# Scale rows by a store to DRAM and a repeating load instead of products with the identity, and one turn of the stabiliser instead of four, in a one-layer encoder kernel

## The chip, the cores and the metric

The kernel runs on one core of one Trainium2 chip. The metric is the device time of one execution in microseconds (us), and its median over several runs. The core has five engines that run their own instruction streams in a fixed order: TensorE (PE in the profile), VectorE (DVE), ScalarE (ACT), GpSimd (POOL) and SyncE (SP), which issues nearly all DMA transfers of this kernel. An engine waits at an instruction until the semaphores it names have been raised; nothing behind it on that engine overtakes it.

## The reference

One layer over 2048 tokens of width 1024, in float32:

```python
xn = rms_norm(x, mix_norm_g)
aq, ak, av, mq, mk, mv, mo, i, f, ga, gm = split(xn @ w_in)
att = chunk_band_attention(aq, ak, av, rel_bias)          # 8 heads of 64, own chunk of 64 and 8 before
hm  = mlstm_chunkwise(silu(conv(mq)), silu(conv(mk)), mv, i + b_i, f + b_f)   # 4 heads of 128, running-max stabiliser
m   = sigmoid(mo) * headwise_rms_norm(hm)
y   = sigmoid(ga) * (att @ w_att_proj) + sigmoid(gm) * (m @ w_mlstm_proj)
x   = x + y @ w_out
x   = x + relu(rms_norm(x, ffn_norm_g) @ w_up) ** 2 @ w_down
out = rms_norm(x, final_norm_g)
```

`rms_norm(x, g)` is `x * rsqrt(mean(x * x) + 1e-6) * g` over the 1024 features of a token.

## The kernel before, in words

**Layout.** The 2048 tokens are four blocks (b = 0 to 3) of T = 512; two blocks are a span (s = 0, 1). Activations lie feature by token: a tile holds 128 features (its partitions) by 512 tokens. A value that belongs to a token, such as the scale of a norm, is then needed as a *row*: the same 512 numbers in each of the 128 partitions. It comes out of a sum over features as a *column*: a tile of 128 x 4, where partition p and column t hold token 128 t + p.

**Products.** Each float32 matrix product is made of three products of rounded parts. ACT rounds a tile into the high part and DVE subtracts it for the low part (`split_now`, lines 585 and 587, for weights; lines 1393 and 1398 for activations). The big products are done by a scheme with seven products in place of eight, with sums of weights that are made on the way and parked in DRAM (`wsum`). Weights flow through four raw tiles (`wraw`) and three split tiles (`wsp`), which PE uses in turn.

**Stages, by time.** The two first blocks' norms and their value products; the input projections of span 0 (`quad`, line 715) up to about 450 us, while the operands of span 1 are prepared (`take_x1`, line 1993, needs the rows of span 1); from 450 us the input products of span 1 (`product`, lines 746 and 751) beside the mixers of blocks 0 and 1, that is attention (lines 1625, 1657, 1550) and recurrence (1874 to 1939); then output projection, up-projection and down-projection (lines 646 to 648) of span 0 with the mixers of blocks 2 and 3 beside it (1450 to 1900 us); then the same for span 1, whose last block is turned to token by feature for its final norm (`down_turned`, line 1017; `turned`, `turned_out`).

**The four places that the change touches.**
- `rows_far(s)`: for each of the span's two blocks, waits for the column of scales `r_in` (the power -0.5 is done by POOL, line 1317 for span 0, line 1339 for span 1), then makes the row by four products of the column, repeated over 128 columns, with the identity (line 1352). ACT copies the bank into a `bias` tile (line 1355).
- `final_scale(s, h)`: the same for the final norm of blocks 0, 1 and 2: sums over features by four products with ones (line 2672), a scale on DVE (2675), the power on POOL (2679), four products with the identity (2683), a copy by ACT (2686). `final_put` then multiplies eight tiles by the row on DVE (2658) and sends them out.
- `turned(s, mid)` for block 3: loads the row of mean squares of the middle norm, `midd` (line 2613, in `final_mid`), squares it on ACT (2615), and turns it to a column by four products with ones (2522) and a scale on DVE (2525).
- `gates_rest(b)`: the stabiliser `mt`, a tile of 128 tokens by 16 (four groups of tokens by four heads), is turned to rows by four turns of 4 columns each (line 1806), copied by ACT as 4 x 512 (1809) and stored to DRAM (`mrow`), from where the recurrence loads a head's row for all partitions (`load_rec`, line 1835).

**What sets the order.** Every piece of work is a generator that yields the engine it wants next with an estimated duration (`yield "pe", 1080`). A planner (`Flow`) runs all generators once against estimated clocks, takes due times from that run, and runs them again to emit the instructions in planned order. A store or load yields 800 ns of the SP queue and some time until it counts as landed. So other costs, or other pieces of work, change the order of everything planned later, on all engines; the hardware then keeps that order.

Of the kernel before, what the change touches and what calls it, by code (L numbers as in the profile page):

```python
# [38 lines left out]
EPS = 1e-6  # L39
# [93 lines left out]
class Flow:  # L133
# [162 lines left out]
def act_ns(n, ps=False, ap=0):  # L296
    return (51 if ps else 93) + 0.834 * n + 93 * ap
# [16 lines left out]
class Layer:  # L314
# [1027 lines left out]
    def rows_far(self, s, ready, read):  # L1342

        fl, nc = self.fl, self.nc
        got = yield "get", self.bias, 2
        yield "wait", [self.ev_const]
        for b in range(2):
            yield "wait", [self.ev_r[2 * s + b]]
            (bk,) = yield "get", self.banks, 1
            yield "pe", 1080  # L1350
            for t in range(NT):
                nc.tensor.matmul(bk[:, t * P:(t + 1) * P], self.rin[2 * s + b][:, t:t + 1].to_broadcast([P, P]),
                                 self.ident, start=True, stop=True)
            yield "act", act_ns(512, True)
            nc.scalar.copy(got[b][:, :T], bk)
            fl.put(self.banks, bk)
            self.rows[b] = got[b][:, :T]
        fl.set(ready)
        yield "wait", read
        fl.put(self.bias, *got)  # L1360

    def square_in(self, b, k, x, tot, ev):

# [356 lines left out]
    def gates_rest(self, b, bk):  # L1720
        fl, nc, B, sm = self.fl, self.nc, self.blk[b], self.sm
        V = nc.vector
# [7 lines left out]
        e, d, s, s2, p = (sm[n] for n in ("e", "d", "s", "s2", "p"))  # L1730
# [30 lines left out]
        a, z = self.cum  # L1761
# [3 lines left out]
        while sh < P:  # L1765
            yield "dve", 150
            V.tensor_tensor(z[:, 64:], a[:, 64:], a[:, 64 - sh:192 - sh], op=ALU.max)
            a, z = z, a
# [4 lines left out]
                         start=True, stop=True)  # L1773
# [27 lines left out]
        V.tensor_scalar(ex[:, 1], ex[:, 1], 0.5, None, op0=ALU.mult)  # L1801
        yield "dve", 85
        V.tensor_scalar(ex[:, 2], ex[:, 2], C1, None, op0=ALU.mult)
        yield "pe~", 428
        for c in range(NT):
            nc.tensor.transpose(bk[:MH, c * P:(c + 1) * P], sm["mt"][:, c * MH:(c + 1) * MH], self.ident)
        (tmp,) = yield "get", self.temp, 1
        yield "act", act_ns(512, True)
        nc.scalar.copy(tmp[:MH, :512], bk[:MH])
        fl.put(self.banks, bk)  # L1810
        fl.set(B["gates"])
        fl.spawn(self.store(self.mtd.ap()[b], tmp[:MH, :512], B["rows"], self.temp, tmp), 1)

    def recurrence(self, b):
        fl, B = self.fl, self.blk[b]
# [663 lines left out]

    def final(self, s):  # L2480
        fl = self.fl
        tot, mid = yield "get", self.bias, 2
        fl.spawn(self.turned(s, mid), 2)
# [21 lines left out]
        fl.put(self.temp, sq)  # L2505
        fl.set(summed[j])

    def turned(self, s, mid):

        fl, nc = self.fl, self.nc  # L2510
        V = nc.vector
        yield "wait", [self.acc_done[s][4, 1], self.kept_ev]
        self.tgain = [g[:, :512] for g in (yield "get", self.temp, 2)]
        yield "sp", 1570, 2000
        for o in range(2):
            nc.sync.dma_start(self.tgain[o], self.io["grow"][:, o * 512:o * 512 + 512].to_broadcast([P, 512]))
        ev = Event()
        yield from self.final_mid(2 * s + 1, mid[:, :512], ev)
        (bk,) = yield "get", self.banks, 1
        yield "pe~", 900  # L2520
        for t in range(NT):
            nc.tensor.matmul(bk[:, 2 * t:2 * t + 2], mid[:, t * P:(t + 1) * P], self.ones, start=True, stop=True)
        r, sums = self.rr["z3"], self.rq
        yield "dve", 150
        V.tensor_scalar(r, bk[:, :2 * NT].rearrange("p (t a) -> p t a", a=2)[:, :, 0], 1.0 / D, None, op0=ALU.mult)
        fl.put(self.banks, bk)
        fl.put(self.bias, mid)
        done = [Event() for _ in range(2 * NT)]
        for o in (4, 0):
            for t in range(NT):  # L2530
                fl.spawn(self.turn_part(s, o, t, done[t + (4 - o)]), 2)
        yield "wait", done
        yield "dve", 150
        V.scalar_tensor_tensor(r, sums[:, 0], 1.0 / D, r, op0=ALU.mult, op1=ALU.add)
        fl.set(self.turned_ev)
# [130 lines left out]
    def final_scale(self, s, h, slot, summed, ready):  # L2666
        fl, nc = self.fl, self.nc
        yield "wait", summed
        (bk,) = yield "get", self.banks, 1
        yield "pe~", 900  # L2670
        for t in range(NT):
            nc.tensor.matmul(bk[:, 2 * t:2 * t + 2], slot[:, t * P:(t + 1) * P], self.ones, start=True, stop=True)
        r = self.rr[f"z{2 * s + h}"]
        yield "dve", 75
        nc.vector.tensor_scalar(r, bk[:, :2 * NT].rearrange("p (t a) -> p t a", a=2)[:, :, 0], 1.0 / D, None,
                                op0=ALU.mult)
        fl.put(self.banks, bk)
        yield "pool", 1900
        nc.gpsimd.tensor_tensor(r, r, self.half, op=ALU.pow)
        (bk,) = yield "get", self.banks, 1  # L2680
        yield "pe~", 1080
        for t in range(NT):
            nc.tensor.matmul(bk[:, t * P:(t + 1) * P], r[:, t:t + 1].to_broadcast([P, P]), self.ident,
                             start=True, stop=True)
        yield "act", act_ns(512, True)
        nc.scalar.copy(slot[:, :512], bk)
        fl.put(self.banks, bk)
        fl.set(ready)

    def late(self):  # L2690
# [11 lines left out]
    def build(self):  # L2702
        fl, nc = self.fl, self.nc
        E = lambda n: [Event() for _ in range(n)]
        f32d = lambda name, *shape: nc.dram_tensor(name, shape, F32, kind="Internal")
# [11 lines left out]
        self.xud = f32d("xu", 7, 4, P, T)  # L2717
        self.gated, self.mtd = f32d("gatepart", 40, T), f32d("mrow", NB, MH, T)
        self.rbd = f32d("relrow", AH, 512)
        self.fin_ev = [E(KT) for _ in range(2)]  # L2720
        self.fin = [f32d(f"fin{h}", KT, P, T) for h in range(2)]
        self.ud = f32d("u", 4, 7, 4, P, T)
# [18 lines left out]
        for b in range(NB):  # L2741
# [3 lines left out]
                mid=Event(), vo={}, vn={}, vp_ev=E(4), mvh_ev=E(MH), row_ev=E(MH), rows=Event(), gf=Event(), heads_left=[2] * 4))  # L2745
# [115 lines left out]
```

## Time and profile before

| | |
|---|---|
| median of 3 runs | 2727.39 us (2727.08 to 2732.34) |
| profiled execution: its span | 2725.8 us, first to last instruction |
| around the span | 2727.4 - 2725.8 = 1.6 us to the median |
| DMA | 678 MB, 249 GB/s over the span |
| granted TensorE clock | 0.999 |

How to read the views. The profile is of one execution. "Busy" is the time in which an engine had an instruction under way; on PE, products overlap, so two starts are closer together than a product is long. A row of instruction groups names the line of the kernel, engine and operation, output <- inputs by the program's tile names, shapes, count, busy time, mean duration in ns of one, and the idle time ahead of them with what ended it. A float32 product that is not split in parts shows as two records, so four products with the identity are "x8", and four turns are "x4". A row of waits reads: who waited <- for what: total us, times, longest. "[1.11 <-DVE ctx L2086]" behind a row of the timeline is idle time ahead of it and its releaser. "Us to landing" of a DMA is counted from its issue.

### The profile page before, as it was taken

The page shows a single profiled execution, that of the slowest core. Times are in us where ns is not written, and L with a number is a line of the kernel's source. Part 1 is how long each engine was busy: PE and PEld are TensorE (multiplying, and loading weights), DVE is VectorE, ACT ScalarE, POOL GpSimd, SP SyncE. Part 2 cuts the span into 40 slices and gives each one's busy share as a digit, 9 for nine tenths or more (in the row PEclk, how much of TensorE's full clock was granted, in tenths as well). Part 3 has the DMA queues.
Part 4 walks back from the last instruction along what each step waited for, and adds up shares of the span by engine and source line. Part 5 has one row for each costly group of instructions (what it writes and reads, how often), then busy time and mean ns, then how long its engine had stood idle before and what let it go on. Part 6 is the DMA issues. An engine that isn't in the chain of part 4 may idle for free.

```text
span 2725.8 us, 38104 instructions
## 1 busy us (share of the span) xinstructions
PE 2708.3 (99%) x12784; PEld 2253.3 (83%) x12784; DVE 2108.8 (77%) x3750; ACT 1542.1 (57%) x2685; POOL 48.0 (2%) x79
## 2 busy tenths in 40 slices
PE   9999999999999999999999999999999999999998
PEld 8878888888888887888888888888888888888887
DVE  7878876888877879987768888889798665657675
ACT  6545456776753645566556766656345565554443
POOL 0000000000000000000000000000000000000000
PEclk9999999999999999999999999999999999999999
DMA  8777889888877889867779787776864454578773
GB/s 305 275 258 277 301 286 293 272 242 275 262 234 238 270 302 321 286 214 265 266 236 288 244 257 225 240 232 220 276 227 160 163 197 159 189 271 285 274 239 134
DMA packets 336712, 678.29 MB, mean 249 GB/s; under 512 B 37396, under 2 KB 66708, under 8 KB 336516
## 3 DMA queue, kind: packets, MB, share of 16 engines
q1 hardware_dynamic: 335796, 674.80, 74.1%
q8 instruction: 100, 1.64, 0.3%
q10 hardware_dynamic: 720, 1.06, 0.1%
q14 instruction: 96, 0.79, 0.1%
HBM read 458.27 MB, written 214.30 MB: 247 GB/s over the span
## 4 chain that ended last, share of the span: by engine, by line
PE 86%; DVE 7%; DMA 3%; issue 2%; ACT 2%; SPq 0%; POOL 0%; ACTq 0%; POOLq 0%; DVEq 0%
PE bank L715 34%; PE bank L746 11%; PE bank L647 8%; PE bank L648 8%; PE bank L646 8%; PE bank L1181 3%; PE bank L751 2%; PE bank L1550 2%; PE bank L1625 2%; PE bank L1657 2%; DVE wsp L587 1%; PE bank L1017 1%; DMA tmp<-in_x 1%; DMA x<-ctx 1%; PE bank L1885 0%
## 5 line engine op out<-in xcount | busy, mean ns | idle before, releaser
L715 PE MATMUL bank<-r,wsp 128*128 128x512 f32 x4872 | 1111.3, 390 | 2.2 <-DVE ctx L2086 1.1
L715 PEld LDWEIGHTS bank<-r,wsp 128*128 128x128 f32 x4872 | 913.0, 188 | 195.0 <-DVE ctx L2086 3.5
L585 ACT CAST wsp<-wraw 128x1024 fp32r<-128x1024 f32 x437 | 459.1, 1051 | 491.4 <-PE bank L715 167.8
L587 DVE TENSOR_TENSOR wsp<-wraw,wsp 128x1024 fp32r<-128x1024 f32 x437 | 534.0, 1222 | 239.0 <-ACT wsp L585 233.7
L646 PE MATMUL bank<-r,wsp 128*128 128x512 f32 x960 | 379.3, 395 | 0.0
L648 PE MATMUL bank<-r,wsp 128*128 128x512 f32 x960 | 375.3, 391 | 0.0
L647 PE MATMUL bank<-r,wsp 128*128 128x512 f32 x960 | 375.2, 391 | 0.0
L746 PE MATMUL bank<-r,wsp 128*128 128x512 f32 x1512 | 368.6, 394 | 0.9 <-DVE ctx L941 0.7
L746 PEld LDWEIGHTS bank<-r,wsp 128*128 128x128 f32 x1512 | 279.0, 188 | 56.9 <-DVE ctx L941 1.6
L648 PEld LDWEIGHTS bank<-r,wsp 128*128 128x128 f32 x960 | 180.2, 188 | 38.5
L647 PEld LDWEIGHTS bank<-r,wsp 128*128 128x128 f32 x960 | 180.5, 188 | 33.4
L646 PEld LDWEIGHTS bank<-r,wsp 128*128 128x128 f32 x960 | 180.4, 188 | 33.5
L1398 DVE TENSOR_TENSOR r<-r 128x512 fp32r<-128x512 f32 x255 | 167.9, 684 | 20.6 <-ACT r L1393 20.0
L2086 DVE TENSOR_TENSOR ctx<-bank,ctx 128x512 f32<-128x512 f32 x174 | 118.9, 686 | 70.3 <-PE bank L715 67.5
L1393 ACT CAST r<-r 128x512 fp32r<-128x512 f32 x255 | 148.8, 617 | 33.4 <-DMA r<-u 30.4
L604 DVE TENSOR_TENSOR wraw<-wraw,wraw 128x1024 f32<-128x1024 f32 x112 | 136.4, 1218 | 4.3 <-DMA wsum<-wraw 3.3
L1638 ACT ACTIVATE sc<-sc,scs 128x640 f32<-128x640 f32 (+4 forms) x128 | 97.6, 763 | 67.5 <-DVE scs L1631 66.5
L2078 ACT COPY ctx<-bank 128x512 f32<-128x512 f32 x174 | 100.9, 583 | 61.0 <-PE bank L715 43.4
L2407 ACT ACTIVATE ctx<-ctx 128x512 f32<-128x512 f32 x96 | 60.6, 631 | 103.2 <-DVE ctx L2086 103.1
L1662 DVE TENSOR_TENSOR r<-bank,r 128x512 fp32r<-128x512 f32 (+1 forms) x168 | 95.7, 593 | 15.0 <-ACT r L1660 14.4
L1550 PE MATMUL bank<-r,r 128*128 128x512 f32 x336 | 94.8, 364 | 0.0
L1660 ACT CAST r<-bank 128x512 fp32r<-128x512 f32 (+1 forms) x168 | 81.0, 516 | 17.2 <-PE bank L1657 16.0
(267 smaller groups left out, 3253.3 us busy)
## 6 DMA issues: line engine op xcount, KB each, us to landing
wraw<-in_wf SPq DMA_DIRECT2D x196, 512.0 KB, 4.9
r<-u SPq DMA_DIRECT2D x224, 256.0 KB, 4.3
wraw<-wsum SPq DMA_DIRECT2D x104, 512.0 KB, 4.6
u<-ctx SPq DMA_DIRECT2D x128, 256.0 KB, 2.4
ctx<-in_wf SPq DMA_DIRECT2D x104, 256.0 KB, 4.4
wsum<-ctx SPq DMA_DIRECT2D x104, 256.0 KB, 4.2
u<-tmp SPq DMA_DIRECT2D x96, 256.0 KB, 2.7
ctx<-in_xt SPq DMA_DIRECT2D x64, 256.0 KB, 4.8
```

The costliest lines, as they stand in the source:

```text
L585: nc.scalar.copy(w[:, 0], raw)
L587: nc.vector.tensor_sub(w[:, 1], raw, w[:, 0].bitcast(F32))
L604: V.tensor_sub(dst, x, y)
L646: mm(ps, lh, rh, start=first, stop=False)
L647: mm(ps, lh, rl, start=False, stop=False)
L648: mm(ps, ll, rh, start=False, stop=last)
L715: mm(ps, wv[:, x, k, n], a[:, y], start=new and k == 0 and x == y == 0, stop=k == 3 and x == 1, skip_group_check=True)
L746: mm(ps, wv[:, x, k, n], a[:, y], start=start and x == y == 0, stop=stop and x == 1, skip_group_check=True)
L1393: self.nc.scalar.copy(dst[:, 0], src)
L1398: self.nc.vector.tensor_sub(dst[:, 1], src, dst[:, 0].bitcast(F32))
L1550: nc.tensor.matmul(bkv[:, :, c0:c0 + w], st, sl[:, :, o:o + w], start=n == 0, stop=n == total - 1)
L2086: nc.vector.tensor_add(t[:, o:o + 512], ps, t[:, o:o + 512])
```

## The change

Four edits:
1. `row_of`, a new helper, stores a column (128 x 4) to a row of 512 numbers in DRAM, `tokrow`, waits for that store, and loads the row into all 128 partitions. `rows_far` uses it for span 1 in place of the products with the identity (span 0 keeps them).
2. `final_scale` uses it for its three rows.
3. `turned` loads the row of `midd` straight as a column, and squares it on DVE with the factor EPS; the row load, the square on ACT, the four products with ones and the scale on DVE go, and so does the use of a second `bias` tile.
4. `gates_rest` turns all 16 columns of `mt` at once; ACT copies 16 x 128, and the store puts the pieces in place.

```diff
@@ rows_far
             yield "wait", [self.ev_r[2 * s + b]]
+            if s == 1:
+                yield from self.row_of(self.rin[2 + b], self.rowd.ap()[b:b + 1], got[b][:, :T])
+                self.rows[b] = got[b][:, :T]
+                continue
             (bk,) = yield "get", self.banks, 1
...
+    def row_of(self, r, row, to):
+        kept = Event()
+        yield from self.store(row.rearrange("o (t p) -> p (o t)", p=P), r, kept)
+        yield "wait", [kept]
+        yield "sp", 800, 2500
+        self.nc.sync.dma_start(to, row.to_broadcast([P, T]))
@@ gates_rest
-        yield "pe~", 428
-        for c in range(NT):
-            nc.tensor.transpose(bk[:MH, c * P:(c + 1) * P], sm["mt"][:, c * MH:(c + 1) * MH], self.ident)
+        yield "pe~", 107
+        nc.tensor.transpose(bk[:16, 0:P], sm["mt"], self.ident)
         (tmp,) = yield "get", self.temp, 1
-        yield "act", act_ns(512, True)
-        nc.scalar.copy(tmp[:MH, :512], bk[:MH])
+        yield "act", act_ns(128, True)
+        nc.scalar.copy(tmp[:16, :P], bk[:16, 0:P])
...
-        fl.spawn(self.store(self.mtd.ap()[b], tmp[:MH, :512], B["rows"], self.temp, tmp), 1)
+        fl.spawn(self.store(self.mtd.ap()[b].rearrange("h (c p) -> c h p", p=P), tmp[:16, :P], B["rows"],
+                            self.temp, tmp), 1)
@@ turned
-        ev = Event()
-        yield from self.final_mid(2 * s + 1, mid[:, :512], ev)
-        (bk,) = yield "get", self.banks, 1
-        yield "pe~", 900
-        for t in range(NT):
-            nc.tensor.matmul(bk[:, 2 * t:2 * t + 2], mid[:, t * P:(t + 1) * P], self.ones, start=True, stop=True)
         r, sums = self.rr["z3"], self.rq
+        yield "wait", [self.blk[2 * s + 1]["mid"]]
+        yield "sp", 800, 2000
+        nc.sync.dma_start(r, self.midd.ap()[2 * s + 1, 0].rearrange("(t p) -> p t", p=P))
         yield "dve", 150
-        V.tensor_scalar(r, bk[:, :2 * NT].rearrange("p (t a) -> p t a", a=2)[:, :, 0], 1.0 / D, None, op0=ALU.mult)
-        fl.put(self.banks, bk)
-        fl.put(self.bias, mid)
+        V.scalar_tensor_tensor(r, r, EPS, r, op0=ALU.mult, op1=ALU.mult)
@@ final_scale
-        (bk,) = yield "get", self.banks, 1
-        yield "pe~", 1080
-        for t in range(NT):
-            nc.tensor.matmul(bk[:, t * P:(t + 1) * P], r[:, t:t + 1].to_broadcast([P, P]), self.ident,
-                             start=True, stop=True)
-        yield "act", act_ns(512, True)
-        nc.scalar.copy(slot[:, :512], bk)
-        fl.put(self.banks, bk)
+        n = 2 + 2 * s + h
+        yield from self.row_of(r, self.rowd.ap()[n:n + 1], slot[:, :512])
```

The changed kernel's line numbers are higher: by 4 to 11 from `rows_far` on. Its line 2664 is line 2658 of before (the scales of `final_put`), 2681 is 2675, 2540 is 2534, 2342 is the store at 2331, 1371 is the new repeating load, 1668, 1636 and 1561 are 1657, 1625 and 1550, and 1911, 1913 and 1915 are 1900, 1902 and 1904.

How the order moves, at three places. The first is the end of DVE's order, where the weights of the last quarter of `down_turned` are split (L587) and block 2's eight output tiles are scaled (L2658, reading the row in `bias_96`). Before:

```order
L2675 TENSOR_SCALAR r_z_180<-bank_135 128x4
L2534 SCALAR_TENSOR_TENSOR r_z_181<-r_q,r_z_181 128x4
L587 TENSOR_TENSOR wsp_61<-wraw_67,wsp_61 128x1024
L587 TENSOR_TENSOR wsp_62<-wraw_64,wsp_62 128x1024
L2658 SCALAR_TENSOR_TENSOR ctx_125<-ctx_125,gcol,bias_96 128x512
L2658 SCALAR_TENSOR_TENSOR ctx_128<-ctx_128,gcol,bias_96 128x512
```

In the changed kernel, the same place on DVE:

```order
L2681 TENSOR_SCALAR r_z_180<-bank_129 128x4
L587 TENSOR_TENSOR wsp_61<-wraw_67,wsp_61 128x1024
L2540 SCALAR_TENSOR_TENSOR r_z_181<-r_q,r_z_181 128x4
L2664 SCALAR_TENSOR_TENSOR ctx_120<-ctx_120,gcol,bias_96 128x512
L2664 SCALAR_TENSOR_TENSOR ctx_119<-ctx_119,gcol,bias_96 128x512
L2664 SCALAR_TENSOR_TENSOR ctx_122<-ctx_122,gcol,bias_96 128x512
L587 TENSOR_TENSOR wsp_62<-wraw_64,wsp_62 128x1024
L2664 SCALAR_TENSOR_TENSOR ctx_114<-ctx_114,gcol,bias_96 128x512
```

Three scales now stand ahead of the split of `wraw_64`; in both kernels the rest of the eight scales and then the split of `wraw_65` follow.

The second place is SP's order near the second row of span 1 in the changed kernel (`r_in_174` is block 3's column, `bias_97` the tile for its row); before, nothing of this passed through SP.

```order
L2342 DMA wsum<-ctx_114 128x512
L2342 DMA tokrow<-r_in_174 128x4x1
L531 DMA wraw_67<-in_wf 128x1024
L2342 DMA gate<-ctx_116 128x512
L1371 DMA bias_97<-tokrow 128x512
L2342 DMA gate<-ctx_125 128x512
L517 DMA ctx_117<-in_wf 128x512
```

Two transfers stand between the store and the load that waits for it, and the later ones wait behind that load.

The third place is PE's order in the mixers of block 0, among the input products (L746): turns of the weights of attention (L1657), products with the values (L1550), scores of the next head (L1625) and recurrence (L1900 to L1904). Before:

```order
L1657 MATMUL bank_131<-const,sc_101 128x128
L1550 MATMUL bank_130<-r_72,r_91 128x512
L1550 MATMUL bank_130<-r_72,r_91 128x2x128
L1625 MATMUL bank_129<-r_75,r_80 128x128 x2
L746 MATMUL bank_133<-r_95,wsp_63 128x512 x3
L1900 MATMUL bank_135<-ctx_113,ctx_115 128x129
```

In the changed kernel:

```order
L1668 MATMUL bank_131<-const,sc_101 128x128 x2
L1636 MATMUL bank_130<-r_75,r_80 128x128 x2
L746 MATMUL bank_129<-r_95,wsp_63 128x512 x3
L1911 MATMUL bank_136<-ctx_113,ctx_119 128x129
L1913 MATMUL bank_136<-ctx_113,ctx_115 128x129
L1915 MATMUL bank_136<-cst_146,r_90 128x129
L746 MATMUL bank_129<-r_69,wsp_63 128x512 x3
L1561 MATMUL bank_132<-r_72,r_91 128x512
L1561 MATMUL bank_132<-r_72,r_91 128x2x128
```

The products with the values (L1561) have moved behind the recurrence's and two more groups of input products. Shifts of this kind run through both stretches with mixers, 450 to 850 us and 1450 to 1900 us.

More of the change, by code (lines that the diff above doesn't have):

```diff
@@ L2481, in final @@
         fl = self.fl
-        tot, mid = yield "get", self.bias, 2
-        fl.spawn(self.turned(s, mid), 2)
+        (tot,) = yield "get", self.bias, 1
+        fl.spawn(self.turned(s), 2)
         summed, ready, sent = [Event() for _ in range(KT + 1)], Event(), []
@@ L2506, in final1, with turned @@
         fl.set(summed[j])
-    def turned(self, s, mid):
+    def turned(self, s):
         fl, nc = self.fl, self.nc
@@ L2719, in build @@
         self.rbd = f32d("relrow", AH, 512)
+        self.rowd = f32d("tokrow", 5, T)
         self.fin_ev = [E(KT) for _ in range(2)]
```

## The prediction

> **What bounds the kernel now.** I read the page first, for who is busy.
>
> ```profile
> span 2725.8 us, 38104 instructions
> PE 2708.3 (99%) x12784; PEld 2253.3 (83%) x12784; DVE 2108.8 (77%) x3750; ACT 1542.1 (57%) x2685; POOL 48.0 (2%) x79
> PE 86%; DVE 7%; DMA 3%; issue 2%; ACT 2%; SPq 0%; POOL 0%; ACTq 0%; POOLq 0%; DVEq 0%
> ```
>
> TensorE (PE) is busy for 99% of the span, and the chain that ended last runs through it for 86%. So each instruction taken from PE is worth its own time, as long as PE's input stays ready. How often it is not ready today is what the table of stages tells (core time, busy time of each engine, granted clock, DMA share, GB/s).
>
> ```profile
> 0.00:100.00 100.00, 97.95 (x442) 81.43 (x443) 82.80 (x140) 61.61 (x98) 2.69 (x6) 1.00 0.85 302
> 100.00:450.00 350.00, 348.66 (x1549) 284.23 (x1548) 267.44 (x408) 178.38 (x279) 6.15 (x6) 1.00 0.81 281
> 450.00:850.00 400.00, 398.23 (x2121) 336.88 (x2120) 311.65 (x800) 259.33 (x571) 14.93 (x28) 1.00 0.83 262
> 850.00:1450.00 600.00, 598.26 (x2632) 491.91 (x2631) 493.50 (x691) 327.15 (x482) 0.10 (x1) 1.00 0.78 264
> 1450.00:1900.00 450.00, 448.02 (x2394) 381.63 (x2394) 383.47 (x952) 305.23 (x634) 15.58 (x30) 1.00 0.78 245
> 1900.00:2700.00 800.00, 799.70 (x3571) 662.75 (x3570) 561.59 (x749) 400.47 (x605) 6.33 (x4) 1.00 0.64 217
> 2700.00:2726.00 26.00, 17.50 (x86) 14.45 (x84) 8.33 (x16) 9.93 (x20) 2.18 (x4) 0.89 0.31 115
> ```
>
> Columns after the stage's length: PE, PE's weight loads, VectorE (DVE), ScalarE (ACT), GpSimd (POOL). Stage length less PE's busy time gives PE's idle time: 2.1 us at the start, then 1.3, 1.8, 1.7, 2.0 and 0.3 us, so 7.1 us between 100 and 2700 us. The clock was granted in full (1.00). The last row puts PE's last product at about 2717.5 us, with 8.3 us of tail behind it. The first two of the waits of PE, longest first, show what that idle time is made of.
>
> ```profile
> PE bank L1657 <- ACT sc L1645: 1.4, 3, 1.0
> PE bank L715 <- DVE ctx L2086: 1.1, 1, 1.1
> ```
>
> The numbers are the total, how often, and the longest: single stops of up to a microsecond. No steady shortage exists. The time can therefore move in two ways: PE gets less work, or the new order has more, or fewer, of these stops.
>
> **The products that go.** From the chain, the scale product of the final norm (L2683) and the turned sums of the last block (L2522):
>
> ```profile
> 2492.80 0.89 PE bank L2683 x8
> ```
>
> ```profile
> 2634.29 0.79 PE bank L2522 x8
> 2635.08 0.35 PE bank L646
> 2635.42 0.23 PE bank L647
> ```
>
> From the timeline of PE, the row products of the second span (L1352) and the stabiliser's turns (L1806), with a single turn of the new shape (L1760):
>
> ```profile
> 243.78 1.05 PE L1352 MATMUL bank<-const,r_in 128*128 128x128 f32 x8
> 244.59 5.72 PE L715 MATMUL bank<-r,wsp 128*128 128x512 f32 x24
> ```
>
> ```profile
> 173.92 0.60 PE L1806 MATMUL bank<-const,g_mt 128*4 128x128 f32 x4
> 174.27 3.00 PE L715 MATMUL bank<-r,wsp 128*128 128x512 f32 x12
> ```
>
> ```profile
> 157.55 0.27 PE L1760 MATMUL bank<-const,g_u 128*16 128x128 f32 x1
> 157.57 2.76 PE L715 MATMUL bank<-r,wsp 128*128 128x512 f32 x11
> ```
>
> Durations overlap on PE, so I count from start to start, plus the 0.1 us by which the product behind such a group is slower (0.35 for 0.23 at L646).
> - L2683: 0.89 us, three times (two blocks of the first span, one of the second): 2.7.
> - L1352, second span: 244.59 - 243.78 = 0.81, plus 0.1, so 0.9, twice: 1.8.
> - L2522: 0.79 + 0.12 = 0.9, once.
> - L1806: 174.27 - 173.92 = 0.35, plus 0.1, so 0.45 for four turns; one turn of a 16-column tile as at L1760 is 0.02 + 0.1 = 0.12. That saves 0.33 in each of four blocks: 1.3.
>
> Sum: 2.7 + 1.8 + 0.9 + 1.3 = 6.7 us, all on PE, all on the path. The copies of ACT that go with them (L1355, L2686) and one square (L2615) save nothing: ACT is at 57%, and neither of the two waits above names them.
>
> **What is added: five rows by DRAM.** Each is a store of 512 single floats and a load of 256 KB that must wait for it. The load waits on SP, in whose queue all other transfers stand behind it. No store of single floats is in this trace, so I bound it.
>
> ```profile
> q1 hardware_dynamic: 335796, 674.80, 74.1%
> wsum<-ctx SPq DMA_DIRECT2D x104, 256.0 KB, 4.2
> tmp<-in_xt SPq DMA_DIRECT2D x20, 256.0 KB, 5.6
> ctx<-mrow SPq DMA_DIRECT2D x16, 256.0 KB, 3.5
> out_x<-ctx SPq DMA_DIRECT2D x12, 256.0 KB, 2.0
> ```
>
> A packet of the SP queue takes 0.741 x 2725.8 x 16 / 335796 = 96 ns of one DMA engine on average. 512 packets on 16 engines are 32 each, at most 3.1 us if a 4-byte packet is as slow as a mean one. Low end: it is as quick as the quickest store, 2.0 us from issue to landing. So 2.0 to 5.1 us in a quiet queue; I take 3, nearer the low end, because 2 KB move in all. The repeating load is like `ctx<-mrow`: 3.5 us, 2.0 when nothing else runs.
>
> [...]
>
> *The two rows of the second span (near 180 and 245 us).* Behind the second store one 512 KB load and one gate store stand ahead of the dependent load, so SP stands for perhaps 2 us. On DVE, eleven instructions (three L587, one L604, seven 512-column ones) lie between L1337, which gives POOL its input, and the first use of the second row.
>
> ```profile
> L587 DVE TENSOR_TENSOR wsp<-wraw,wsp 128x1024 fp32r<-128x1024 f32 x437 | 534.0, 1222 | 239.0 <-ACT wsp L585 233.7
> L604 DVE TENSOR_TENSOR wraw<-wraw,wraw 128x1024 f32<-128x1024 f32 x112 | 136.4, 1218 | 4.3 <-DMA wsum<-wraw 3.3
> L2086 DVE TENSOR_TENSOR ctx<-bank,ctx 128x512 f32<-128x512 f32 x174 | 118.9, 686 | 70.3 <-PE bank L715 67.5
> 179.71 1.49 POOL L1339 TENSOR_TENSOR r_in<-r_in,half 128x4 f32<-128x4 f32 x1 [134.43 <-DVE r_in L1337]
> 233.61 3.18 POOL L1339 TENSOR_TENSOR r_in<-r_in,half 128x4 f32<-128x4 f32 x1 [52.40 <-DVE r_in L1337]
> 215.45 0.17 DVE L2244 COPY ctx<-hist 128x3 f32<-128x3 f32 x1 [3.37 <-DMA wsum<-ctx]
> 220.11 2.11 PE L715 MATMUL bank<-r,wsp 128*128 128x512 f32 x8 [1.11 <-DVE ctx L2086]
> ```
>
> Their work is 4 x 1.22 + 7 x 0.69 = 9.7 us. The round trip is the power on POOL (1.5 to 3.2), a store (2.0 to 4.2) and a load (3.5 to 5.6): 7.0 to 13.0 us. So DVE stands for 0 to 3.3 us, and behind it wait a weight split and the sums that clear PE's banks. The trace has this very case: DVE stood for 3.37 us on a transfer at 215 us, and PE stood for 1.1 us at 220. Cost 0 to 1.1 us; I take 0.6, the middle. If the row came early it could not gain, since PE does not wait for it today.
>
> *The two rows of the first span's final norm (near 2490 and 2565 us).* SP stands for a store's landing, twice. PE's idle time there is 0.3 us in 800, DMA is at 0.64, and operands and weights lie loaded ahead. Zero; without that cover, the 3 us of a store each time.
>
> *The last row, near 2690 us,* has no such cover, because the kernel ends there.
>
> ```profile
> 2688.40 1.99 POOL L2679 TENSOR_TENSOR r_z<-r_z,half 128x4 f32<-128x4 f32 x1 [122.31 <-DVE r_z L2534]
> 2694.16 1.23 DVE L587 TENSOR_TENSOR wsp<-wraw,wsp 128x1024 fp32r<-128x1024 f32 x1 [4.64 <-ACT wsp L585]
> 2695.30 5.38 DVE L2658 SCALAR_TENSOR_TENSOR ctx<-ctx,gcol,bias 128x512 f32<-128x512 f32 x8
> 2701.60 15.90 PE L1017 MATMUL bank<-wsp,r 128*128 128x512 f32 x69
> ```
>
> Today DVE splits the weights of the last quarter (L587) and then scales eight tiles (L2658). In the new order three scales stand ahead of the first of the last two splits and five ahead of the second. POOL is done at 2690.4. Store (2.0 to 5.1), load (2.0 to 3.5) and 0.4 for issue put the scales at 2694.8 to 2699.4, against 2695.3 today. Three scales of 0.67 and a split of 1.23 finish the first weights at 2698.0 to 2702.6; five scales and a split more finish the second at 2702.6 to 2707.2. PE's last quarter is 48 products at 15.9 / 69 = 0.23 us, 11 us, so it begins at 2706.6, and needs the second tile six products later, at 2708.0; both 0.9 earlier without L2683, so 2705.7 and 2707.1. The cost is 0 to 0.1: nothing, and no gain either if the row comes sooner, since PE's products set the end. What decides is whether the two transfers together take more than 2707.1 - 2690.4 - 0.4 - 2 x 1.23 - 8 x 0.67 = 8.5 us.
>
> *Everything else.* The stabiliser's row goes out in 16 runs of 512 bytes instead of 4 of 2 KB, the turned block's mean row comes in as 512 single floats long before it is used, some 10 more DMAs and 1 MB of 678 MB: zero, hidden beside PE. The planner, fed other costs, also deals the attention and recurrence stages in another order, as the rows of PE show; PE does the same products there, so only the stops can change.
>
> **Sum.** -6.7 + 0.6 = -6.1 us. The profiled span is 2725.8, 1.6 under the median of 2727.4; the same 1.6 lies around it afterwards: 2727.4 - 6.1 = 2721.3 us, a span of 2719.7. About 0.2% (5.5 us) is what a measurement of this kernel can tell from no change, so even the plain case is barely visible.
>
> **Rivals.**
> 1. *Gain kept, stops as now* (the forecast): 2713.6, if all 7.1 us of stops also went, to 2721.9. For it: PE never waits on what is replaced. Chance 0.47.
> 2. *The new order gives the gain back.* In the mixers (450 to 850 and 1450 to 1900 us) DVE is busy for 78 and 85%, and every product there sits close behind the ACT or DVE result it needs; a shuffled order has other stops, of half a microsecond to one each by the two waits above. With 1.2 to 12.2 us more of them: 2721.9 to 2732.9, no change. For it: the order moves over hundreds of rows. Against it: the same planner with the same rules holds the stops at 7.1 us now. Chance 0.37.
> 3. *The same, worse:* more than 12.2 us of new stops, 2.7 times today's; 2733 to 2740, slower. Chance 0.12.
> 4. *The scattered store is slow, and the end waits.* Place: DVE's three scales ahead of the last two splits. Every microsecond over 8.5 for store and load is one at the end; slower than now by over 0.2% from 8.5 + 6.7 + 5.5 = 20.7 us on. Were all 512 packets on one DMA engine at 96 ns, the store would take 49 + 2 us: the two transfers 54, and 54 - 8.5 - 6.7 = 39 us are lost there alone, 2766. Against it: 128 rows can be dealt to 16 engines. Chance 0.04. [...]
>
> **Numbers.** Faster 0.47 (case 1), same 0.37 (case 2), slower 0.16 (cases 3 and 4). Range 2714 to 2733: from case 1's low end to where case 3 begins; case 1's own is 2713.6 to 2721.9.
>
> **What would show it.** Right: L2522 and L2683 gone, about 6.7 us less of PE's work, PE's idle time between 100 and 2700 us within a few microseconds of 7.1, the last scales starting 4.4 to 9.0 us behind the end of the last row's power on POOL, no wait of L1017 on L587. Wrong: a wait of L1017 on L587 near the end; stops of PE in 450 to 850 or 1450 to 1900 well over 1.8 and 2.0 us; a store of the row that lands more than 5 us after its issue in the quiet end.

## The result, and the profile after

The changed kernel takes 2754.4 us (median of 4 runs, 2753.3 to 2756.8) beside 2729.1 us for the kernel before (4 runs, 2727.1 to 2732.3): a ratio of 1.0088, 95% interval 1.0076 to 1.0101. It is 25 us slower. The forecast was 2721.3 us and the range ended at 2733.

The page of the changed kernel, the same three lines as before:

```profile
span 2753.2 us, 37966 instructions
PE 2711.4 (98%) x12724; PEld 2251.8 (82%) x12724; DVE 2113.0 (77%) x3749; ACT 1538.8 (56%) x2680; POOL 45.4 (2%) x79
PE 83%; DVE 6%; DMA 5%; issue 4%; ACT 2%; SPq 0%; POOL 0%; POOLq 0%; DVEq 0%; ACTq 0%
```

PE has 60 instructions fewer and is busy for 3.1 us *more*. The table of stages (columns as in the prediction) shows where it stands:

```profile
100.00:450.00 350.00, 337.90 (x1474) 274.94 (x1473) 261.28 (x398) 169.11 (x261) 3.96 (x5) 0.98 0.79 268
450.00:850.00 400.00, 391.74 (x2081) 329.72 (x2080) 309.43 (x796) 262.55 (x581) 15.40 (x29) 1.00 0.83 259
850.00:1450.00 600.00, 595.53 (x2623) 490.11 (x2622) 485.19 (x668) 317.27 (x466) 0.00 (x0) 1.00 0.79 266
1450.00:1900.00 450.00, 447.28 (x2350) 379.23 (x2349) 378.67 (x931) 300.79 (x618) 15.83 (x30) 1.00 0.78 242
1900.00:2700.00 800.00, 799.16 (x3580) 662.71 (x3579) 573.13 (x786) 410.54 (x632) 4.34 (x4) 1.00 0.66 222
```

Stage length less PE's busy time is now 12.1, 8.3, 4.5, 2.7 and 0.8 us, where it was 1.3, 1.8, 1.7, 2.0 and 0.3. That is 21.3 us more, half of it (10.8) in the first row, where the clock has also fallen, to 0.98. The waits of PE, and two of SP's queue (the first from 100 to 450 us, the second from 2700 us to the end), name the places:

```profile
PE bank L715 <- DVE ctx L2097: 9.6, 3, 7.2
PE bank L715 <- ACT ctx L2089: 3.2, 1, 3.2
PE bank L1017 <- DVE wsp L587: 3.1, 2, 2.8
PE bank L1636 <- DVE scs L1642: 2.5, 3, 1.0
```

```profile
SPq L1371 <- DMA tokrow<-r_in: 15.0, 2, 8.7
```

```profile
SPq L1371 <- DMA tokrow<-r_z: 9.0, 1, 9.0
```

L1371 is the repeating load of a row, held until the scattered store has landed. How one such wait becomes a stop of PE can be followed in three timelines: SP's, DVE's and PE's near the second row.

```profile
254.06 0.40 SPq L2342 DMA_DIRECT2D tokrow<-r_in  x1
254.56 1.56 SPq L531 DMA_DIRECT2D wraw<-in_wf  x1
256.21 0.43 SPq L2342 DMA_DIRECT2D gate<-ctx  x1
265.41 0.32 SPq L1371 DMA_DIRECT2D bias<-tokrow  x1
```

```profile
271.42 0.69 DVE L522 TENSOR_TENSOR ctx<-ctx,ctx 128x512 f32<-128x512 f32 x1 [8.93 <-DMA ctx<-in_wf]
```

```profile
272.76 12.46 PE L715 MATMUL bank<-r,wsp 128*128 128x512 f32 x43 [7.23 <-DVE ctx L2097]
```

The store goes out at 254.06 and the load at 265.41, so the store took about 11 us. Behind the load stood the weights that DVE's L522 needs (`ctx<-in_wf`). DVE stood for 8.93 us, then PE for 7.23, since DVE clears its banks. The restart is slow as well. The third figure from the end of these rows, the granted clock, shows it:

```profile
266.00:272.00 6.00, 0.00 (x0) 0.00 (x0) 0.58 (x1) 0.00 (x0) 0.00 (x0) 0.65 0.92 262
272.00:276.00 4.00, 3.23 (x8) 2.56 (x9) 4.00 (x6) 1.12 (x2) 0.00 (x0) 0.50 0.79 303
276.00:280.00 4.00, 4.00 (x15) 3.22 (x14) 1.92 (x3) 1.54 (x2) 0.00 (x0) 0.75 0.74 290
```

From 272 to 276 us PE is granted half its clock and starts 8 products in 3.23 us, where the full clock has 15 (45 or 46 in 10 us). Summed in steps of 1 us, PE's busy time multiplied by the part of the clock that was not granted comes to 7.3 us in this run and to 0.0 in the kernel before. That is most of what lies between PE's busy time and the one forecast (3.1 + 6.7 = 9.8 us). It is lost in three places: 1.6 us behind a stop of 3.2 us near 209 us, 2.6 us here, and 3.1 us at the end, which the rows below show. The 0.75 over 276 to 280 us puts the return of the full clock at about 278, 5 us behind the restart. The two shorter stops were followed by half the clock as well: it is 0.50 from 210 to 213 us, and 0.50 in the 6 us behind the stop of 2.8 us at the end.

The last row, at the end of the kernel, has such a stop too. Its store goes out at 2710.91 us. Here are DVE's wait for the row, PE's wait for the weights that DVE splits behind it, and the stage after that, with the granted clock again third from the end:

```profile
2725.11 2.08 DVE L2664 SCALAR_TENSOR_TENSOR ctx<-ctx,gcol,bias 128x512 f32<-128x512 f32 x3 [13.84 <-DMA bias<-tokrow]
```

```profile
2732.82 12.46 PE L1017 MATMUL bank<-wsp,r 128*128 128x512 f32 x41 [2.79 <-DVE wsp L587]
```

```profile
2733.00:2739.00 6.00, 6.00 (x15) 4.64 (x16) 1.55 (x3) 1.21 (x3) 0.55 (x1) 0.50 0.05 20
```

PE starts 15 products in these 6 us, where the full clock has 27 or 28.

My first theory from this comparison was that the waits do it: SP stands for 6.3, 8.7 and 9.0 us at these three rows, some 15 us are lost at the two rows of the second span and 6.6 at the end, and the new order adds some 10 us of stops in the mixers. The rival was that the new order does it all, the other edits among it.

### The profile page after: what moved, and what is told of

The parts are those of the page before. It is cut to its first block, busy times and chain, and to the rows that moved or that the text cites. A ratio compares the mean times of both kernels' runs of the same rounds, so it can differ in the third digit from the quotient of the medians.

```text
span 2753.2 us, 37966 instructions
## 1 busy us (share of the span) xinstructions
PE 2711.4 (98%) x12724; PEld 2251.8 (82%) x12724; DVE 2113.0 (77%) x3749; ACT 1538.8 (56%) x2680; POOL 45.4 (2%) x79
## 4 chain that ended last, share of the span: by engine, by line
PE 83%; DVE 6%; DMA 5%; issue 4%; ACT 2%; SPq 0%; POOL 0%; POOLq 0%; DVEq 0%; ACTq 0%
PE bank L715 36%; PE bank L746 9%; PE bank L648 8%; PE bank L647 8%; PE bank L646 8%; PE bank L1181 3%; PE bank L751 2%; PE bank L1561 2%; PE bank L1636 1%; PE bank L1017 1%; PE bank L1668 1%; DVE wsp L587 1%; DVE sc L1642 1%; DMA r<-kfar 1%; DMA wsum<-wraw 1%
## 5 line engine op out<-in xcount | busy, mean ns | idle before, releaser
L587 DVE TENSOR_TENSOR wsp<-wraw,wsp 128x1024 fp32r<-128x1024 f32 x437 | 533.9, 1222 | 211.7 <-ACT wsp L585 196.5
L746 PE MATMUL bank<-r,wsp 128*128 128x512 f32 x1512 | 367.6, 394 | 4.2 <-DVE r L1673 2.4
L746 PEld LDWEIGHTS bank<-r,wsp 128*128 128x128 f32 x1512 | 278.7, 188 | 59.9 <-DVE r L1673 3.0
L604 DVE TENSOR_TENSOR wraw<-wraw,wraw 128x1024 f32<-128x1024 f32 x112 | 136.7, 1221 | 12.5 <-DMA wsum<-wraw 11.4
L1561 PE MATMUL bank<-r,r 128*128 128x512 f32 x336 | 96.2, 367 | 2.3 <-DVE r L1673 1.0
L1636 PE MATMUL bank<-r,r 128*128 128x256 f32 (+2 forms) x464 | 89.9, 313 | 3.0 <-DVE scs L1642 2.5
```

Source lines behind the costliest of these rows:

```text
L587: nc.vector.tensor_sub(w[:, 1], raw, w[:, 0].bitcast(F32))
L604: V.tensor_sub(dst, x, y)
L746: mm(ps, wv[:, x, k, n], a[:, y], start=start and x == y == 0, stop=stop and x == 1, skip_group_check=True)
L1561: nc.tensor.matmul(bkv[:, :, c0:c0 + w], st, sl[:, :, o:o + w], start=n == 0, stop=n == total - 1)
```

## The experiments

Times of the kernel before are those beside each set of runs: 2729.2 us for runs 1 to 4, 2730.8 for runs 5 to 8, 2730.2 for runs 9 to 12. They stand within 0.06% of each other. The edits are shown cut short, with "..." for what is left out; each run has one trace.

**1. The load waits for nothing.**

```diff
-        self.nc.sync.dma_start(to, row.to_broadcast([P, T]))
+        self.nc.sync.dma_start(to, self.io["one"].to_broadcast([P, T]))
...
```

> The repeating load of each of the five rows reads a constant input row of ones in place of the row just stored, so it waits for no store; the scattered stores of 512 floats still go out. Leaves out the scales of the second span's rows and of the final norm (ones in their place). PE, DVE, ACT and POOL keep the changed kernel's order, SP's alone moves. Theory (the wait for the scattered store's landing, 8 to 9 us each, costs some 15 us at 200 to 300 us and 6.6 us at the end): the time falls by 18 to 24 us, to 2730 to 2737 us; what stays above the kernel before is the new order's stops, some 10 us, less 6.7 us of PE work. Rival (the stops come from the new order of the instructions and would stand there without the wait): 2748 us or more.

Measured: 2744.6 us, ratio 1.0062 (1.0047 to 1.0077). Both missed. The wait was worth 9.8 us of the 25.3; 15.4 stayed, with no wait of L1371 left. What stayed is in the movement of data. In these rows of 186 to 196 us, the last two figures are the DMA share and GB/s; first the kernel before, then the changed one, then this one:

```profile
186.00:196.00 10.00, 10.00 (x50) 8.41 (x49) 5.82 (x7) 4.85 (x10) 0.00 (x0) 1.00 0.93 316
```

```profile
186.00:196.00 10.00, 10.00 (x46) 8.29 (x45) 5.98 (x8) 4.17 (x8) 0.71 (x1) 1.00 0.26 47
```

```profile
186.00:196.00 10.00, 10.00 (x46) 8.29 (x45) 5.79 (x8) 4.50 (x7) 0.52 (x1) 1.00 0.28 52
187.90:190.90 3.00, 3.00 (x15) 2.49 (x14) 1.61 (x4) 1.33 (x2) 0.00 (x0) 1.00 0.03 11
```

And from its DMA view, the packets of 186.5 to 188.0 us, and, of those issued from 186 to 187.5 us, the store and its neighbour:

```profile
DMA packets 536, 0.01 MB, mean 7 GB/s; under 512 B 532, under 2 KB 532, under 8 KB 536
```

```profile
tmp<-in_xt SPq DMA_DIRECT2D x1, 256.0 KB, 12.1
tokrow<-r_in SPq DMA_DIRECT2D x1, 2.0 KB, 10.0
```

The packets of the 2 KB store are through by 188 us. Then, for three microseconds, almost nothing moves (11 GB/s), and the rate over the ten is a sixth of before, although SP has issued several transfers of 256 and 512 KB by then. The load of 256 KB issued next lands 12.1 us after its issue. Nobody waits for the store; the traffic stands with it. So the theory fell in its main part, and I formed another: the store itself holds back the core's transfers for about 10 us, and the wait on SP comes on top.

**2. Fewer and longer pieces.**

```diff
-        yield from self.store(row.rearrange("o (t p) -> p (o t)", p=P), r, kept)
+        yield from self.store(row.rearrange("o (p t) -> p (o t)", p=P), r, kept)
```

> The row store writes 128 runs of 16 bytes in place of 512 singles of 4 bytes (the row lies in another order in DRAM, so the scales are permuted); the wait and the load stay, and PE, DVE, ACT and POOL keep the changed kernel's order. Theory, landing goes with the number of separate writes (some 16 ns each): the store lands in 3.5 to 5 us instead of 9 to 11, the stops at 205, 265 and 2720 us shrink by 5 to 6 us each, 2737 to 2744 us. Rival order: 2750 us or more. Rival fixed cost (a store through DRAM with a wait lands that late whatever its pieces): landing still 9 us, 2754 us.

Measured: 2730.5 us, ratio 1.0006 (0.9997 to 1.0016): 24 us of the 25 are gone, more than I expected, with the wait in place and every engine, SP's transfers too, in the changed kernel's order. Only the form of the five stores differs. From its view of `tokrow`, and two of its stages:

```profile
DMA to landing us min/median/max: 3.8/3.8/3.9
```

```profile
100.00:450.00 350.00, 348.69 (x1544) 284.97 (x1543) 269.12 (x408) 178.99 (x278) 4.25 (x6) 1.00 0.81 281
450.00:850.00 400.00, 392.42 (x2077) 329.62 (x2076) 309.69 (x795) 255.68 (x567) 14.85 (x28) 1.00 0.83 258
```

The trace names the landing of one store, 3.8 us (the 3.9 is a load's); the five loads go out 1.5 to 6.4 us behind their stores, where the changed kernel has 9.5 to 11.4. PE's idle time from 100 to 450 us is back at 1.3 us, so waits of this length cost nothing there. From 450 to 850 us it is still 7.6, and that is the new order's: 5.8 us more than before. It is no accident of one trace: the four traces with this order on PE (the changed kernel, runs 1 to 3) have 7.6 to 8.4 us there, and the four with the order of before (the kernel before, runs 9 to 11) 1.8 to 4.1.

**3. The floats apart.** The 512 singles go to 512 places, 512 bytes from each other.

```diff
-        self.rowd = f32d("tokrow", 5, T)
+        self.rowd = f32d("tokrow", 5, T, P)
...
-        self.nc.sync.dma_start(to, row.to_broadcast([P, T]))
+        self.nc.sync.dma_start(to, self.io["one"].to_broadcast([P, T]))
+        self.nc.sync.dma_start(to[:, :1], row[:, :1, 0].to_broadcast([P, 1]))
...
```

> The 512 singles go to 512 separate stretches of 512 bytes instead of one of 2 KB; the load of the row reads a constant row of ones, and a small second load (one float to each of 128 partitions) waits for the store. Leaves out the scales of the second span and of the final norm. If the landing is slow since neighbouring floats share a stretch of DRAM (one write after another to the same place), the store lands in 5 us or less here; if it goes with the number of writes, it lands in 9 to 11 us as before.

One run: 2735.7 us, so the time alone says little. The rate behind the first store, and the landing of the three stores for which the trace names one:

```profile
186.00:196.00 10.00, 10.00 (x46) 8.28 (x45) 5.95 (x8) 4.61 (x7) 0.00 (x0) 1.00 0.80 273
```

```profile
DMA to landing us min/median/max: 2.4/3.5/3.6
```

There are as many writes of 4 bytes as in the changed kernel, and they hold nothing back for long. So the number of small writes is not the cause. What is left is that they share a place, which run 11 tests again.

**4. Turn the column first.** One turn on PE makes 4 rows of 128, ACT copies them, and four runs of 512 bytes are stored.

```diff
-        yield from self.store(row.rearrange("o (t p) -> p (o t)", p=P), r, kept)
...
+        self.nc.tensor.transpose(bk[:NT, :P], r, self.ident)
...
+        self.nc.scalar.copy(tmp[:NT, :P], bk[:NT, :P])
...
+        yield from self.store(row.rearrange("o (t p) -> (o t) p", p=P), tmp[:NT, :P], kept, self.temp, tmp)
```

> The column of 4 x 128 scales is turned by one PE transpose (128x4 to 4x128), copied by ACT, and stored in 4 runs of 512 bytes; wait and repeating load stay. Adds a turn and a copy for each of five rows, and the order of all engines moves. Theory (few long runs land fast): the store lands in 2 to 3 us, SP stands 2 to 4 us at each row instead of 8 to 10, the end's stop at DVE falls from 13.8 to about 7 us with PE's wait there near 0; 2725 to 2742 us, by what the new order happens to cost. Rival (waiting through DRAM costs as much whatever the store): 2750 us or more, with landings of 8 us.

Measured: 2725.4 us, ratio 0.9985 (0.9976 to 0.9995). The changed kernel's idea with this one repair is slightly faster than the kernel before. The loads of the rows go out 1.3 to 3.2 us behind their stores. DVE's stop at the last row is 1.2 us, for 13.8 in the changed kernel (who waited for `tokrow`, us, times):

```profile
DVE ctx L2671: 1.2, 1
```

**5 to 8. The four edits one by one**, each on the kernel before.

> The kernel before with the second span's two rows alone taken through DRAM (scattered store of 512 floats into 2 KB, wait, repeating load). Revised theory (512 floats written one by one into one 2 KB stretch hold back every transfer of the core for about 10 us, whether or not anything waits for the store): two such stores at 185 and 255 us, where DMA is 0.8 busy and PE lives on arriving weights, cost 10 to 16 us, less 1.8 us of products taken off PE: 2737 to 2744 us, with PE idle 9 to 15 us more between 100 and 450 us. Rival (the loss comes from the other three edits or from any new order): 2727 to 2732 us.

> The kernel before with the final norm's three rows alone taken through DRAM. Revised theory: the two stores at about 2500 and 2590 us meet a stage with DMA 0.64 busy and weights read well ahead and cost under 1 us; the last, near 2700 us, has nothing to move at the time but its own load, and costs its landing and the load's on the way to the last rows, some 6 to 8 us, less 2.7 us of products: 2731 to 2736 us. Rival (the end waits for something else anyway): 2725 to 2728 us.

> The kernel before with the stabiliser's edit alone: one 128x16 turn in place of four, ACT's copy of 16x128, the store in 16 runs of 512 bytes. Theory: 1.3 us of turns less, and the attention stage's order redrawn, so that 3 to 6 us of stops come in there (2731 to 2734 us). Rival (the edit keeps its gain): 2726 to 2728 us.

> The kernel before with the transposed mean's edit alone: 512 single floats read from DRAM into 128x4 and squared on DVE, in place of the sums' second copy and 4 products. Reads of single floats held nothing back in the changed kernel's trace (the load landed 4.9 us after its issue, with DMA busy around it). Theory: the order hardly moves; 0 to 1 us less, 2728 to 2730 us. Rival (single floats hold back the traffic when read as well): 2733 us or more.

| edit alone | time, us | ratio | 95% interval |
|---|---|---|---|
| 5. second span's two rows | 2754.9 | 1.0087 | 1.0070 to 1.0104 |
| 6. final norm's three rows | 2731.4 | 1.0001 | 0.9992 to 1.0011 |
| 7. one turn of the stabiliser | 2732.9 | 1.0010 | 1.0001 to 1.0020 |
| 8. block 3's mean row as a column | 2729.0 | 0.9993 | 0.9984 to 1.0002 |

The two rows of the second span alone lose 24.1 us, nearly all that the whole change loses, and 11 more than the upper end of what I expected. (The four differences, 24.1, 0.6, 2.1 and -1.8 us, add up to 25.0.) Their stage and the longest wait of PE, from run 5:

```profile
100.00:450.00 350.00, 333.61 (x1451) 270.38 (x1450) 255.97 (x390) 164.15 (x252) 4.24 (x5) 0.98 0.78 261
```

```profile
PE bank L715 <- DVE ctx L2097: 16.4, 4, 6.8
```

Run 6 stores three such rows where less traffic is needed, and loses nothing that can be measured. Its time lies at the edge of the expected range, but not for the reason given there. The last row was to cost 6 to 8 us, and PE waits 0.6 us for it. PE's busy time falls by 1.9 us of the 2.7 forecast, and against that stands a stop of 2.3 us in another place, near 2647 us, where PE's L2555 waits for L2532 in DVE's order. At its end DVE does stand for the row, but PE waits little (rows of DVE, then PE):

```profile
2701.83 4.06 DVE L2665 SCALAR_TENSOR_TENSOR ctx<-ctx,gcol,bias 128x512 f32<-128x512 f32 x6 [10.17 <-DMA bias<-tokrow]
```

```profile
2709.55 9.60 PE L1017 MATMUL bank<-wsp,r 128*128 128x512 f32 x41 [0.60 <-DVE wsp L587]
```

Run 7 comes closest to the order's price by itself, though its interval nearly reaches 1: PE's idle time from 450 to 850 us is 4.6 us for 1.8, with one stage's row to show it:

```profile
450.00:850.00 400.00, 395.36 (x2100) 333.60 (x2099) 310.51 (x796) 255.13 (x566) 15.22 (x27) 1.00 0.82 258
```

Over 100 to 2700 us PE is idle for 3.8 us more than before, of the 3 to 6 expected. Run 8 reads 512 single floats from one 2 KB stretch and loses nothing, as expected. Its trace does not name the landing of that read (in the changed kernel it is 4.9 us), but the traffic goes on: it goes out at 2396.9 us, and from 2400 to 2408 us 219 GB/s move, where the kernel before has 230. In the changed kernel, where it goes out at 2420.3 us, it is 288 GB/s up to 2422, 277 up to 2425 and 224 up to 2431. Reading them is harmless here, writing them is not.

**9 to 11. The bare store.** The kernel before, complete, plus two stores that nobody reads:

```diff
             yield "wait", [self.ev_r[2 * s + b]]
+            if s == 1:
+                nc.sync.dma_start(self.rowd.ap()[b:b + 1].rearrange("o (t p) -> p (o t)", p=P), self.rin[2 + b])
             (bk,) = yield "get", self.banks, 1
...
```

Run 10 has `nc.scalar` in place of `nc.sync`; run 11 has rows with a pitch of 16 floats (64 bytes) and stores to the first of each.

> The kernel before, complete, with two more transfers on SP's queue: each row of scales of the second span is also stored as 512 single floats into one 2 KB stretch that nobody reads or waits for. PE, POOL and (but for a split repeat) DVE and ACT keep the kernel before's order. Revised theory (the store itself holds back the core's transfers for about 10 us each): 12 to 20 us slower, 2742 to 2750 us, with DMA below 100 GB/s for 8 to 10 us behind each store and PE idle between 195 and 280 us. Rival (it takes the wait, or the new order, to lose time): 2729 to 2732 us.

> The same two unread stores, issued by ACT on its own DMA queue; SP's list of transfers is that of the kernel before, item by item. If the hold-back lies in the issuing queue alone, SP's transfers go on and the time is 2729 to 2733 us. If it lies in the 16 DMA engines or the memory that both queues share, SP's transfers stand as well and the time is that of the run with SP's queue, within 4 us. [...]

> The same two unread stores on SP's queue, but every float goes to a place of its own 64 bytes from the next (512 floats over 32 KB instead of 2 KB). If what is slow is many writes into the same 64 bytes, the traffic goes on as in the run with 512 bytes between the floats: low rate for 2 us, 2729 to 2733 us. If the stretch that writes share is longer than 64 bytes (or the count of single writes decides), it stays slow: 2740 us or more.

Measured: run 9 2743.4 us, ratio 1.0050 (1.0035 to 1.0065); run 10 2744.7 us, 1.0056 (1.0040 to 1.0073); run 11 2729.8 us, 0.9999 (0.9990 to 1.0009). The stores go out at 180.4, 181.1 and 180.0 us. Here is what moved from 182 to 190 us, in the kernel before and in runs 9, 10 and 11 (the last figure is GB/s; a share above 1 is of packets that overlap):

```profile
182.00:190.00 8.00, 8.00 (x37) 6.63 (x36) 6.86 (x11) 3.18 (x5) 0.00 (x0) 1.00 0.89 314
```

```profile
182.00:190.00 8.00, 8.00 (x42) 6.75 (x40) 6.01 (x9) 2.69 (x4) 0.00 (x0) 1.00 1.42 33
```

```profile
182.00:190.00 8.00, 8.00 (x38) 6.64 (x37) 6.71 (x11) 2.73 (x4) 0.00 (x0) 1.00 1.20 79
```

```profile
182.00:190.00 8.00, 8.00 (x41) 6.75 (x40) 5.66 (x9) 3.13 (x7) 0.00 (x0) 1.00 0.89 322
```

In run 10 the first two of the eight microseconds still move 230 GB/s; from 184 to 192 us it is 22 to 59. How long SP's own transfers took to land at that time, in runs 9, 10 and 11 (those issued from 178 to 186.6 us):

```profile
qfar<-tmp SPq DMA_DIRECT2D x3, 256.0 KB, 10.7
```

```profile
qfar<-tmp SPq DMA_DIRECT2D x3, 256.0 KB, 11.8
```

```profile
qfar<-tmp SPq DMA_DIRECT2D x3, 256.0 KB, 2.3
```

The time of run 9 is in the theory's range, that of run 10 in its second case, that of run 11 in its first. Two stores of 2 KB, unread and unwaited for, cost 13 to 15 us when their floats are neighbours, and nothing when each has 64 bytes to itself. Runs 9 and 11 differ in this pitch alone, and run 10 keeps the order of the kernel before on every engine. That settles the cause of the main loss. It is not in the issuing queue: with the store on ACT's own queue, SP's transfers stand too, and the time is the same within the intervals. Whether the DMA engines or the memory hold the traffic, these runs don't tell. Run 11 stores as many single floats as run 9, so the sharing of a place matters, not only the size.

**12. The repair without the stabiliser's edit.** Run 4 with the four turns, and their copy and store, of the kernel before.

> The changed kernel with the rows turned on PE and stored in 4 runs of 512 bytes, and with the stabiliser as in the kernel before (four turns). A candidate for the fastest: the stabiliser's edit alone measured 0.1% slower, and the turned rows 0.15% faster with it in. If the two add, 2721 to 2725 us; if the order's stops are drawn anew with every edit, anywhere from 2722 to 2735 us.

Measured: 2722.9 us, ratio 0.9975 (0.9964 to 0.9985). It beats both kernels. It lies in both of the expected ranges, so it does not tell whether the two gains add or the stops were drawn anew. Its page, and its stages from 100 to 850 us:

```profile
PE 2702.7 (99%) x12741; PEld 2247.4 (83%) x12741; DVE 2112.2 (78%) x3751; ACT 1539.4 (57%) x2683; POOL 46.5 (2%) x79
```

```profile
100.00:450.00 350.00, 350.00 (x1553) 286.20 (x1552) 271.14 (x412) 181.63 (x284) 5.06 (x6) 1.00 0.82 286
450.00:850.00 400.00, 397.00 (x2111) 334.40 (x2110) 310.94 (x798) 255.64 (x565) 16.64 (x28) 1.00 0.83 259
```

PE is busy for 5.6 us less than before, and has no stop at all from 100 to 450 us.

## Why the prediction was wrong

- **The scattered store's duration: wrong, and the origin of the loss.** The step that failed is "I take 3, nearer the low end, because 2 KB move in all", with an upper bound of 5.1 us. In the changed kernel the load that waits for the store went out 9.5 to 11.4 us after it. The packets were as quick as I had bounded them: in run 1 they were through 1.3 us after the issue, and took 0.4 us from the first to the last (the bound was 3.1 us). What I left out is the time between the packets and the landing, which is long where the writes share a place: 8.7 us of the 10.0 from issue to landing in run 1.
- **The cost of the second span's rows, "0 to 1.1 us; I take 0.6": measured 24 us** (run 5). I had priced the store as a wait of its own reader on DVE. (The range was also a little narrow: its round trip has 4.2 us as the store's upper end, and with the 5.1 us of the bound DVE would stand for up to 4.2 us instead of 3.3.) The larger mechanism was in none of my cases (the 0.16 for "slower" stood for two others): the store holds back the other transfers (33 GB/s for 314 over 8 us in run 9), at a point where DMA is over 0.8 busy and DVE and PE live on weights as they arrive. By the bare stores (run 9) the hold-back alone is 13 us; the wait on SP, with the weights queued behind the load, adds some 10 (run 1 against the changed kernel: 9.8; run 5 against run 9: 11.5). The 10 is rough, since run 1 takes away all five waits, the last row's too, and run 5 has another order. In the changed kernel 1.6 and 2.6 us of the loss is the slow clock behind the two stops.
- **The first span's two final rows, "zero": right.** Their loads stood on SP until 9.9 and 10.5 us behind the stores' issue in the changed kernel, and PE was idle for only 0.8 us from 1900 to 2700 us. The cover I named, loaded weights and a DMA share of 0.64, held.
- **The last row, "nothing", deciding point 8.5 us: the place was right, the durations wrong.** Store and load took 2725.11 - 2710.91 = 14.2 us, for which the point gives a cost of 14.2 - 8.5 = 5.7. PE waited for L587 twice, 3.1 us in all, and lost 3.1 us more to the half clock behind the second wait, which I had not priced; that the two together come near 5.7 is luck. (The point itself is about 0.1 us too high: 2717.5 less 11 us is 2706.5, not 2706.6.) This is rival 4's place, priced there through a single slow DMA engine, which was not the reason, since the packets were through by 2712.3 us, 1.4 us behind the issue; its 39 us did not come. In run 6's order the same lateness cost PE 0.6 us.
- **PE's work, -6.7 us: right in kind, somewhat too large.** Where no transfer is held back, PE's busy time falls by 3.8 us (run 2) and by 5.4 us (run 4, with five turns more). Which of the four terms is too large, and why run 2 gains less than run 4, stays open.
- **Rival 2, the order gives the gain back: it does, beside the main effect.** Run 2 has the changed kernel's order without the hold-back. Its PE is idle for 13.6 us from 100 to 2700 us where it was 7.1, and it takes as long as the kernel before. So had the store landed as fast as I assumed, this rival, at 0.37, would by run 2 have been the outcome, and not the forecast.
- **"Everything else: zero": right for the mean row (run 8). For the stabiliser, 0.1% slower** (run 7), through the order that its planned costs deal.

Not settled: why neighbouring writes hold up everything. That writes to one place are done one after another is a guess of mine that is not shown: no view shows the memory, and the landings give no steady price for each. Beside other traffic, floats side by side landed in 10.0 us (run 1), runs of 16 bytes in 3.8 (run 2) and floats 512 bytes apart in 3.5 (run 3). At the last row, with little else moving, the load went out 9.5, 1.5 and 2.5 us behind the store (the changed kernel, runs 2 and 3). How long the shared stretch is stays open too: a pitch of 64 bytes is enough to be free of it, and nothing between 4 and 64 bytes was tried but the runs of 16. Nor was it tried whether another core's transfers would stand as well.

## What to carry to other kernels

Price a scattered store by whether its pieces are small and lie side by side, not by its bytes or packets alone, and ask what else is moving while it lands: two such stores of 2 KB cost 13 us with the floats side by side (run 9) and nothing with 64 bytes from one to the next (run 11). If a column must become a row through DRAM, turn it first, so that it goes out in runs of 512 bytes; here a turn and a copy per row made the difference between 0.9% slower and 0.15% faster (0.25% without the stabiliser's edit). And where a planner deals the order, time an edit's order apart from its work: here it was worth as much as the products saved.

## What the runs showed of the hardware

- 512 neighbouring floats written one by one (2 KB in all) cut the core's DMA from 314 GB/s to 33 for 8 us, from SP's queue (run 9), and to 22 to 59 from 184 to 192 us, from ACT's (run 10). With 64 bytes from one float to the next it stayed at 322 (run 11).
- In runs of 16 bytes the same 2 KB landed in 3.8 us (run 2), where single floats took 9.8 to 12.9 (run 1).
- Reading 512 neighbouring floats one by one held nothing back: 224 to 288 GB/s in the 10.7 us behind the read in the changed kernel; from 2400 to 2408 us 219 GB/s in run 8 and 230 in the kernel before.
- A stop of PE of 2.8 us was followed by 6 us of work at a granted clock of 0.50 (15 products for 27 or 28; the changed kernel, 2733 to 2739 us).
- A stop of PE of 7.2 us cost about 2 us more behind it: 23 products started between 272 and 280 us, the first of them at 272.76, where 7.2 us at the full clock hold 33 (45 or 46 in 10 us; the changed kernel).
